# The context layer's matmuls in plain float32, and its weight chunks in one ring with the experts'

## The chip, the cores and the metric

One core of one Trainium2 chip runs the whole program. The metric is the time of one execution on the device in microseconds; the number given for a kernel is the median of its runs. A single execution, taken by the hardware profiler, gives the rows quoted below.

## What is computed

Two models follow one another on 256 tokens of width 1024, all in float32. The first block mixes (an mLSTM and a gated MLP), attends to a memory, and passes through a mixture of 32 experts. The second block runs two layers on that result (the "latent"), and each of them attends to a second sequence, the context, of 256 rows. The context itself passes through the first layer too, and through the key and value part of the second:

```python
x = first_block(...)                     # ... x + hier_moe(rms_norm(x)), 32 experts, top 2 of one group
xc = ctx
for l in range(2):
    x, xc = _layer(x, xc, ..., ctx_out=(l < 1))

# in _layer, for the context:
hc = rmsnorm(xc, norm_g) * (1.0 + scale_c) + shift_c
parts_c = _split_cols(hc @ w_in)         # layer 0: all 2816 columns; layer 1: only k and v
oc_att = silu(parts_c[3]) * _context_attention(qc, kc, vc)
oc_f, oc_c, oc_p = _local_branches(...)  # Fourier, convolution and pooling branches
xc = xc + gate_c * (concat([oc_f, oc_att, oc_c, oc_p]) @ w_out)

# an expert, on its tokens:
(silu(xb @ w_gate[e]) * (xb @ w_up[e])) @ w_down[e]
```

Nothing of the context's layer depends on the first block, so it can run at any time before the latent layers.

## The kernel before

The program has three parts in time: the first block's mixer and attention (to about 300 us), the experts (about 300 to 830 us), and the two latent layers.

**The experts.** Each pair of experts q has 12 chunks of 128x2048 float32 (1 MB): eight for the gate and up weights, four for the down weights. `SEQ` lists the 192 chunks in the order of use: seven units of two pairs (four experts, 32 columns of TensorE each) and two units of one pair. `expert_unit` multiplies gate and up chunks into tiles named `a` (function `hidden`), the down chunks into tiles named `py`. `moe_chunk` loads a chunk, as one transfer or as two of 512 KB, all from SyncE's queue, which issues in order and waits for the buffer's last user. `st_chunk` picks the buffer: for the first 46 chunks (`NROT`) out of up to 19 buffers, several of them in memory of the front part (pools `pm`, `pf`, `px`), which are given back after unit 1 (`LCU`). From chunk 46 on it rotates through eight buffers of the pool `st`: four with the tag `w`, two `wh`, two `wl`.

**Products in two parts.** Wherever accuracy allows no single reduced product, a float32 operand is written as high + low in the type float32r, and a product becomes three matmuls: high with high, high with low, low with high. For a weight chunk `wchunk` does this: a raw chunk (tag `w`), a high copy by ScalarE (tag `wh`, line 141), a low part by VectorE for one half (`wl`, line 143) and by GpSimd for the other (line 146). `split` does the same for small operands. `fm` and `tm` are the two matmul helpers: the weight chunk stationary, or the activations stationary; each does 48 matmuls of 256 columns for a chunk. The experts' matmuls are plain float32.

**The context's layer.** `gen_ctx` is a generator. `feed` advances it by small steps at fixed points of `expert_unit`, so that its work is spread over units 2 to 6; a planner that simulates a time line then sets the final order on each engine. It runs `layer` with s = 1, which the latent layers use with s = 0: `norm_mod` normalises and transposes the input, then come 11 chunks of `w_in2` and four of `w_out2`, one more chunk of layer 1 for its keys and values: 16 chunks of 1 MB. Each goes through `wchunk`, so it holds three of the eight `st` buffers. Its products land in tiles named `f`; the normalised input is `h2h`, `h2l`, the branches' results `y2h`, `y2l` (made by `put`).

Of the kernel before, what the change touches and what calls it, by code (L numbers as in the profile page):

```python
# [9 lines left out]
F32 = mybir.dt.float32  # L10
# [8 lines left out]
P = 128  # L19
# [8 lines left out]
NS = 4  # L28
NROT, LCU = 46, 1
D = 1024  # L30
KT = 8
# [14 lines left out]
def body(ctx: ExitStack, tc: tile.TileContext, I: dict, out: bass.AP, dbg=None):  # L46
# [156 lines left out]
    def fm(w, h, pst):  # L203

        (wh, wl), (hh, hl) = w, h
        p = pst([2, 256])
        for j in range(2):
            c = slice(j * P, (j + 1) * P)
            for k in range(KT):
                mm(p[:, j], wh[:, k, c], hh[:, k], k == 0, False)  # L210
                mm(p[:, j], wh[:, k, c], hl[:, k], False, False)
            for k in range(KT):
                mm(p[:, j], wl[:, k, c], hh[:, k], False, k == KT - 1)
        return p

    def tm(w, h, t, pst, ks=tuple(range(KT))):

        (wh, wl), (hh, hl) = w, h
        p = pst([wh.shape[2]])
        c = slice(t * P, (t + 1) * P)  # L220
# [434 lines left out]
    slots = [(pf, "p%d" % i) for i in range(NPF)] + [(pm, "mh"), (pm, "ml")]  # L655

    def st_chunk(i):
        n = i
        j = i % (NPF + NX + 10)
        if i < NROT and j >= 8:  # L660
            pool, t = slots[j - 8]
            return moe_chunk(*SEQ[i], pool, t, 1)
        i -= 0 if i >= NROT else i - j
        tag = ("w", "wh", "w", "wl")[i % 4]
        return moe_chunk(*SEQ[n], st, tag, 4 if tag == "w" else 2)

# [178 lines left out]
    def norm_mod(lp, src, l, s, pst, hi, lo, pre=None):  # L845

        ys = [lp.tile([P, D], F32, name="yn", tag="yn", bufs=2) for t in range(2)]
        if pre:
            for h in (slice(0, 512), slice(512, D)):
                for t in range(2):  # L850
                    last = nc.vector.tensor_scalar(ys[t][:, h], src[:, t, h], pre[0][t], None, op0=ALU.mult)
        else:
            for t, y in enumerate(ys):
                r = rms_scale(lp, src[:, t], hi[:, 4 * t:4 * t + 4].rearrange("p a b -> p (a b)"))
                nc.vector.tensor_scalar(y, src[:, t], r, None, op0=ALU.mult)
        sc_ = pre[1] if pre else mod_a[l][:, :, s]
        for f in range(KT):
            p = pst([256])
            for t in range(2):
                nc.tensor.transpose(p[:, t * P:(t + 1) * P], ys[t][:, f * P:(f + 1) * P], ident)  # L860
            a_, b_ = sc_[:, f:f + 1], mods[l][:, f, s:s + 1]
            ev = nc.scalar.activation(hi[:, f], p, AF.Identity, scale=a_, bias=b_)
            tf = lp.tile([P, 256], F32, name="tf", tag="gtm", bufs=2)
            if f % 2:
                nc.scalar.activation(tf, p, AF.Identity, scale=a_, bias=b_)
            else:
                nc.vector.tensor_scalar(tf, p, a_, b_, op0=ALU.mult, op1=ALU.add)
            ev2 = nc.vector.tensor_tensor(lo[:, f], tf, hi[:, f], op=ALU.subtract)
            if f == 7:
                late = (ev, ev2)  # L870
        after_norm[0] = ev2
        return [(last, *pre[2]), (pre[2][0], *late)] if pre else [(), ()]
# [36 lines left out]
    def hpair2(lp, n):  # L909
        return (lp.tile([P, KT, 256], F32R, name=n + "h", tag=n + "h"),  # L910
                lp.tile([P, KT, 256], F32R, name=n + "l", tag=n + "l"))

    def layer(lp, l, s, src, pst, ptr, pat, done=None, pre=None, res=None):
        lat = s == 0
        GC = GS = None
        if lat:
            gb, GC, GS = lrows[l], *rot
            if l:
                rope_rows(l, *rot)
        hT = hpair2(lp, "h2")  # L920
        chain = norm_mod(lp, src, l, s, ptr, *hT, pre=pre)
        yield
# [3 lines left out]
        for c in range(2):  # L926
            with ExitStack() as es:

                for i in chain[c] if c or l == 0 else ():
                    es.enter_context(tc.issue_after(i.ins))  # L930
                w = wchunk(w_in[c])
            for t in range(2):
# [6 lines left out]
        def zsilu(c):  # L939
            z = lp.tile([P, 2, 256], F32, name="sz", tag="sz", bufs=2)  # L940
            nc.scalar.activation(z, fm(wchunk(w_in[c]), hT, pst), AF.Silu)
            return z

        def half_sums(c):

            u = lp.tile([P, 2, 256], F32, name="u", tag="u")
            u0 = lp.tile([P, 256], F32, name="u0", tag="gtm", bufs=2)
            w = wchunk(w_in[c])
            nc.scalar.activation(u0, tm(w, hT, 0, pst), AF.Copy)
# [21 lines left out]
        nk = len(keys)  # L971
        yT = hpair2(lp, "y2")

# [4 lines left out]
        def put(f, val):  # L978

            n = val.shape[1]  # L980
            split(val, yT[0][:, f:f + n], yT[1][:, f:f + n])


        for j in range(2):
# [20 lines left out]
            nc.vector.tensor_tensor(sz[:, j], po, sz[:, j], op=ALU.mult)  # L1005
            yield
# [14 lines left out]
        for f in range(2):  # L1021
# [6 lines left out]
            for o, op in ((yf[:, f, 0:130], ALU.add), (yf[:, f, 127:257][:, ::-1], ALU.subtract)):  # L1028
                nc.vector.tensor_tensor(o.rearrange("p (m e) -> p e m", e=2), pc_, sn_, op=op)
        nc.vector.tensor_tensor(sz, yf[:, :, 0:256], sz, op=ALU.mult)  # L1030
        put(0, sz)
        yield

        p = fm(wchunk(w_in[3]), hT, pst)
        up = lp.tile([P, 2, 272], F32, name="up", tag="up")
# [31 lines left out]
        cg = lp.tile([P, 2, 256], F32, name="cg", tag="PT2", bufs=2)  # L1067
        nc.scalar.activation(cg, fm(wchunk(w_in[8]), hT, pst), AF.Copy)
        yield
        p = pst([2, 256])  # L1070
        for a in range(2):
            mm(p[:, a], pwb[l][:, a], dT[:, a], True, True)
            cp = C_PS2 + 2 * l + a
            nc.vector.scalar_tensor_tensor(sz[:, a], p[:, a], col[:, cp:cp + 1], sz[:, a],
                                           op0=ALU.mult, op1=ALU.mult)
        put(6, sz)
        p = fm(wchunk(w_in[9]), hT, pst)
        tp = lp.tile([P, 2, 258], F32, name="tp", tag="PT2", bufs=2)
# [17 lines left out]
        yield  # L1096
        p = fm(wchunk(w_in[10]), hT, pst)
        nc.vector.tensor_tensor(cg, p, cg, op=ALU.mult)
        put(4, cg)
        yield  # L1100
        sq = lp.tile([P, 2, 4], F32, name="sq")
        for c in range(4):
            w = wchunk(I["w_out2"][l, c])
            for t in range(2):
# [19 lines left out]
    def gen_ctx():  # L1124
# [6 lines left out]

        hT = hpair2(lp, "y2")
        norm_mod(lp, xc, 1, 1, psF, *hT, pre=pre)
        yield
        qkv = lp.tile([P, 2, 512], F32, name="qkv", tag="qkv")
        w = wchunk(I["w_in2"][1, 1])
        for t in range(2):
# [507 lines left out]
```

## Time and profile before

| | before |
|---|---|
| median of 3 runs | 1103.26 us (1099.52 to 1105.23) |
| profiled execution | 1105.26 us |
| its span, first to last instruction | 1103.4 us |
| TensorE busy | 1013.0 us (92%) |
| VectorE, ScalarE, GpSimd busy | 504.9, 372.3, 269.3 us |
| read from memory | 314.74 MB, 286 GB/s over the span |

Matmuls are pipelined and overlap, so TensorE's busy share is not a measure of its load: a matmul that is in the array while the next one starts counts for both. The throughput line in 40 slices of 27.6 us shows best which part is which: it stands near 409 GB/s for most of the experts' part, from slice 11 to slice 30. PE is TensorE, PEld its weight loads, DVE VectorE, ACT ScalarE, POOL GpSimd, SP SyncE; a q behind a name is that engine's queue.

### The profile page before, as it was taken

The numbers are of one execution on the slowest core, as the hardware profiler recorded it, in microseconds if no ns is written. First come the engines' busy times: TensorE is split into PE (matmuls) and PEld (weight loads), VectorE is DVE, ScalarE is ACT, GpSimd is POOL, SyncE is SP. The second block draws the span as 40 slices with busy tenths as digits, with TensorE's granted clock in tenths as the row PEclk, the third lists the DMA queues.
The fourth block names the chain that finished last, engine by engine and source line by source line (L and its number), as shares of the span: only waits on it lengthen the run. The fifth ranks groups of instructions, "written<-read, shape, count | busy, mean of one in ns | idle before, by whom it ended". The sixth has DMA issues, their size and how long they took to land.

```text
span 1103.4 us, 19306 instructions
## 1 busy us (share of the span) xinstructions
PE 1013.0 (92%) x7552; PEld 715.1 (65%) x7552; DVE 504.9 (46%) x992; ACT 372.3 (34%) x656; POOL 269.3 (24%) x211
## 2 busy tenths in 40 slices
PE   8999999999898588899989999997898889998998
PEld 7888999989651232643545654542235878988888
DVE  4966844353640141404432421513133777668755
ACT  5576445443100030211311221310014545554452
POOL 3245443234100000400220121111001453436233
PEclk9999999999799799999999999999999889999999
DMA  9657688866799999799679999999995432335231
GB/s 358 248 212 286 254 291 311 323 232 229 273 392 409 372 412 411 305 398 409 231 313 377 391 390 380 406 408 408 408 409 211 142 126 102 129 115 197 72 114 39
DMA packets 74456, 317.07 MB, mean 287 GB/s; under 512 B 8310, under 2 KB 10742, under 8 KB 61308
## 3 DMA queue, kind: packets, MB, share of 16 engines
q1 hardware_dynamic: 71480, 312.61, 74.0%
q10 hardware_dynamic: 2884, 3.21, 0.9%
q8 instruction: 60, 0.98, 0.4%
q14 instruction: 32, 0.26, 0.1%
HBM read 314.74 MB, written 1.05 MB: 286 GB/s over the span
## 4 chain that ended last, share of the span: by engine, by line
PE 33%; DMA 21%; issue 10%; DVE 4%; SPq 2%; POOL 2%; ACT 2%; DVEq 0%; POOLq 0%; ACTq 0%
DMA wm<-moe 21%; PE a L106 19%; PE f L106 7%; PE py L106 3%; PE sc L106 2%; SPq L543 2%; DVE wl L143 1%; PE po L106 1%; ACT wh L141 1%; POOL wl L146 1%; PE t L997 1%; PE t L860 0%; DVE qkv L885 0%; POOL rrow L906 0%; SPq L552 0%
## 5 line engine op out<-in xcount | busy, mean ns | idle before, releaser
L146 POOL TENSOR_TENSOR wl<-w,wh 128x512 fp32r<-128x512 f32 (+1 forms) x158 | 224.4, 1441 | 535.1 <-ACT wh L141 453.8
L106 PE MATMUL a<-wm,xg 128*32 128x512 f32 (+1 forms) x1024 | 219.4, 609 | 15.1 <-DMA wm<-moe 14.8
L141 ACT ACTIVATE wh<-w 128x1024 fp32r<-128x1024 f32 (+1 forms) x158 | 157.0, 1041 | 107.0 <-PE a L106 54.0
L143 DVE TENSOR_TENSOR wl<-w,wh 128x1024 fp32r<-128x1024 f32 (+1 forms) x79 | 107.4, 1359 | 87.6 <-ACT wh L141 86.0
L106 PEld LDWEIGHTS a<-wm,xg 128*32 128x32 f32 (+1 forms) x1024 | 46.8, 113 | 146.7 <-DMA wm<-moe 79.1
L106 PE MATMUL py<-wm,aT 128*32 128x256 f32 (+1 forms) x1024 | 90.1, 398 | 19.4 <-ACT aT L1389 12.6
L106 PEld LDWEIGHTS py<-wm,aT 128*32 128x32 f32 (+1 forms) x1024 | 41.1, 116 | 58.7 <-ACT aT L1389 14.1
L106 PE MATMUL a<-h2l,wh 128*128 128x256 f32 x256 | 67.1, 293 | 0.0
L106 PE MATMUL a<-h2h,wh 128*128 128x256 f32 x256 | 66.5, 292 | 0.0
L1382 DVE SCALAR_TENSOR_TENSOR sg<-a,ws,sg 128x512 f32<-128x512 f32 x9 | 6.8, 751 | 119.2 <-PE a L106 119.2
L106 PEld LDWEIGHTS a<-h2l,wh 128*128 128x128 f32 x256 | 49.6, 194 | 3.6 <-issue 3.5
L106 PEld LDWEIGHTS a<-h2h,wh 128*128 128x128 f32 x256 | 49.7, 194 | 0.8 <-issue 0.7
L106 PE MATMUL a<-hh,wh 128*128 128x256 f32 x192 | 49.0, 291 | 0.3 <-ACT wh L141 0.3
L106 PE MATMUL a<-hl,wh 128*128 128x256 f32 x192 | 47.8, 285 | 0.0
L1389 ACT ACTIVATE aT<-t 128x512 f32<-128x512 f32 x9 | 5.3, 592 | 110.2 <-PE t L1387 78.4
L106 PEld LDWEIGHTS a<-hh,wh 128*128 128x128 f32 x192 | 37.3, 194 | 2.6 <-ACT wh L141 1.7
L1415 DVE SCALAR_TENSOR_TENSOR yl<-py,ws,yh 128x512 fp32r<-128x512 f32 x16 | 12.0, 750 | 56.2 <-ACT yh L1414 56.2
L106 PE MATMUL a<-h2h,wl 128*128 128x256 f32 x256 | 37.7, 284 | 0.0
L106 PEld LDWEIGHTS a<-hl,wh 128*128 128x128 f32 x192 | 37.3, 194 | 0.0
L106 PE MATMUL f<-h2h,wh 128*128 128x256 f32 x128 | 32.8, 292 | 1.8 <-ACT wh L141 1.8
L106 PEld LDWEIGHTS a<-h2h,wl 128*128 128x128 f32 x256 | 33.4, 188 | 0.7 <-issue 0.7
L106 PE MATMUL a<-wh,yh 128*128 128x256 f32 x128 | 33.0, 292 | 0.0
(500 smaller groups left out, 2113.7 us busy)
## 6 DMA issues: line engine op xcount, KB each, us to landing
wm<-moe SPq DMA_DIRECT2D x336, 512.0 KB, 10.1
w<-w_in SPq DMA_DIRECT2D x46, 1024.0 KB, 5.2
w<-w_mod SPq DMA_DIRECT2D x24, 1024.0 KB, 5.0
wm<-moe SPq DMA_DIRECT2D x24, 1024.0 KB, 8.7
w<-w_out SPq DMA_DIRECT2D x16, 1024.0 KB, 5.0
w<-w_kv SPq DMA_DIRECT2D x8, 1024.0 KB, 5.0
w<-w_q SPq DMA_DIRECT2D x4, 1024.0 KB, 8.6
w<-w_o SPq DMA_DIRECT2D x4, 1024.0 KB, 7.1
```

The costliest lines, as they stand in the source:

```text
L106: return nc.tensor.matmul(o, l, r, start=a, stop=b)
L141: nc.scalar.activation(hi[:, a:a + n], raw[:, a:a + n], AF.Copy)
L143: nc.vector.tensor_tensor(lo[:, a:a + n], raw[:, a:a + n], hi[:, a:a + n], op=ALU.subtract)
L146: nc.gpsimd.tensor_tensor(lo[:, a:a + n], raw[:, a:a + n], hi[:, a:a + n], op=ALU.subtract)
L543: nc.sync.dma_start(t[:, e * 1024:(e + 1) * 1024], I["moe"][bass.ds(expert_at(2 * q + e), 1), c].rearrange("a p n -> p (a n)"))
L997: nc.tensor.transpose(pt[:, i], sm[:, i * P:(i + 1) * P], ident)
L1382: nc.vector.scalar_tensor_tensor(sg, pu, ws[:, 1:2], sg, op0=ALU.mult, op1=ALU.mult)
L1389: nc.scalar.activation(aT, pt, AF.Copy)
L1415: nc.vector.scalar_tensor_tensor(yl[:, cs], py[c], ws[:, 0:1], yh[:, cs], op0=ALU.mult, op1=ALU.subtract)
```

## The change

`fm` and `tm` get a second form: if the weight is a single tile, they do one plain float32 matmul where the other form does three. The context's layer uses it throughout: `norm_mod` writes one float32 tile instead of two parts, the branches write into one tile `y2` (`piece`, in place of `put`), and `fchunk` loads a chunk with no copies behind it. The latent layers keep the form in two parts.

`fchunk` takes its buffer from the same rotation as the experts' chunks (`ring`, with a shared counter `used`), and the rotation gets four more buffers, `r0` to `r3`, in memory that is free after unit 1. So there are 12, and a context chunk takes one.

```diff
+NRX = 4
     def fm(w, h, pst):
+        p = pst([2, 256])
+        if not isinstance(w, tuple):
+            for j in range(2):
+                for k in range(KT):
+                    mm(p[:, j], w[:, k, j * P:(j + 1) * P], h[:, k], k == 0, k == KT - 1)
+            return p
...
     def tm(w, h, t, pst, ks=tuple(range(KT))):
+        c = slice(t * P, (t + 1) * P)
+        if not isinstance(w, tuple):
+            p = pst([w.shape[2]])
+            for k in ks:
+                mm(p, h[:, k, c], w[:, k], k == ks[0], k == ks[-1])
+            return p
...
+    def ring(i):
+        if i >= NROT and i % (8 + NRX) >= 8:
+            return slots[-1 - i % (8 + NRX) + 8][0], slots[-1 - i % (8 + NRX) + 8][1], 1
+        i = i % (8 + NRX) if i >= NROT else i
+        tag = ("w", "wh", "w", "wl")[i % 4]
+        return st, tag, 4 if tag == "w" else 2
+
+    used = [NROT]
+
     def st_chunk(i):
-        n = i
         j = i % (NPF + NX + 10)
-        if i < NROT and j >= 8:
+        if i >= NROT:
+            used[0] += 1
+            return moe_chunk(*SEQ[i], *ring(used[0] - 1))
+        if j >= 8:
             pool, t = slots[j - 8]
             return moe_chunk(*SEQ[i], pool, t, 1)
-        i -= 0 if i >= NROT else i - j
-        tag = ("w", "wh", "w", "wl")[i % 4]
-        return moe_chunk(*SEQ[n], st, tag, 4 if tag == "w" else 2)
+        return moe_chunk(*SEQ[i], *ring(j))
+
+    def fchunk(src):
+        pool, tag, n = ring(used[0])
+        used[0] += 1
+        t = pool.tile([P, 2048], F32, name="wc", tag=tag, bufs=n)
+        nc.sync.dma_start(t, src)
+        return t.rearrange("p (k c) -> p k c", k=8)
...
+            if lo is None:
+                if f % 2:
+                    nc.scalar.activation(hi[:, f], p, AF.Identity, scale=a_, bias=b_)
+                else:
+                    nc.vector.tensor_scalar(hi[:, f], p, a_, b_, op0=ALU.mult, op1=ALU.add)
+                continue
...
+        wt = wchunk if lat else fchunk
...
-        hT = hpair2(lp, "h2")
+        hT = hpair2(lp, "h2") if lat else hone(lp, "h2")
...
-                w = wchunk(w_in[c])
+                w = wt(w_in[c])
...
         def put(f, val):
             n = val.shape[1]
-            split(val, yT[0][:, f:f + n], yT[1][:, f:f + n])
+            if lat:
+                split(val, yT[0][:, f:f + n], yT[1][:, f:f + n])
...
+        def piece(f, val):
+            return val if lat else yT[:, f:f + val.shape[1]]
...
         if u == LCU:
             pre.close()
+            rx = mo.enter_context(tc.tile_pool(name="rx", bufs=1, reuse_waits="tile"))
+            slots += [(rx, "r%d" % i) for i in range(NRX)]
```

How this moves the instructions, at three places. First TensorE, at the end of unit 2, where the context layer's first products stand. Of before; `wh` is a chunk's high part, `h2h` and `h2l` the two parts of the normalised context, and the rows with `f` go on in this way to 48 for a chunk:

```order
L1387 MATMUL t<-c_ident,sg 128x128 x4
L106 MATMUL t<-WRp,Pm 32x2 x8
L106 MATMUL py_4561<-wm,aT 32x256 x3
L1360 MATMUL t<-c_ident,Pm 128x128 x2
L106 MATMUL py_4561<-wm,aT 32x256 x29
L106 MATMUL f<-wh,h2h 128x256
L106 MATMUL f<-wh,h2l 128x256
```

The same place now; `wc` is a context chunk as loaded:

```order
L108 MATMUL py_4539<-wm,aT 32x256 x30
L108 MATMUL f<-wc,h_4412 128x256 x16
L108 MATMUL py_4540<-wm,aT 32x256
L108 MATMUL a<-yh,PT 128x512
L108 MATMUL a<-yl,PT 128x512
L108 MATMUL a<-yh,PT 128x512
L108 MATMUL f<-wc,h_4412 128x256 x16
L108 MATMUL py_4540<-wm,aT 32x256 x31
L108 MATMUL f<-h_4412,wc 128x256 x16
```

Each chunk's 48 matmuls have become 16, and they stand at the same points among the experts' matmuls.

Second SyncE, at the first context chunks and the expert chunk behind them, with what each load waits for (a DMAHW name is a place among the loads in flight, the others are engines that used the buffer before). Of before:

```order
L67 DMA w_4608<-w_in2 128x2048 [waits DMAHW5_49,PE_49]
L67 DMA w_4669<-w_in2 128x2048 [waits DMAHW6_49,PE_49]
L543 ISA
L543 DMA wm_4730<-moe 128x1024 [waits DMAHW7_49,PE_49]
L543 ISA
L543 DMA wm_4730<-moe 128x1024 [waits DMAHW0_49]
L543 ISA
L543 DMA wm_4733<-moe 128x1024 [waits DVE_49,PE_49,DMAHW1_49,Activation_49,Pool_49]
```

Now, at the same point of SyncE's order:

```order
L694 DMA wc_4586<-w_in2 128x2048 [waits DMAHW5_49,PE_49]
L694 DMA wc_4608<-w_in2 128x2048 [waits DMAHW6_49,PE_49]
L555 ISA
L555 DMA wm_4630<-moe 128x1024 [waits DMAHW7_49,PE_49]
L555 ISA
L555 DMA wm_4630<-moe 128x1024 [waits DMAHW0_49]
L555 ISA
L555 DMA wm_4633<-moe 128x1024 [waits DMAHW1_49,PE_49]
```

The loads stand in the same sequence, but an expert chunk behind a context chunk now waits for TensorE alone, not for the three engines that made its parts.

Third SyncE, at the context's input `xc`. Of before, at the end of unit 1's loads:

```order
L552 ISA x2
L1129 DMA xc_4406<-ctx 128x1024 [waits DMAHW7_49,PE_49]
L1129 DMA xc_4406<-ctx 128x1024 [waits DMAHW0_49]
L543 ISA
L543 DMA wm_4183<-moe 128x1024 [waits DMAHW1_49,PE_49]
```

Now, among unit 2's loads:

```order
L555 DMA wm_4398<-moe 128x1024 [waits DMAHW1_49]
L555 ISA
L555 DMA wm_4398<-moe 128x1024 [waits DMAHW2_49]
L1176 DMA xc_4409<-ctx 128x1024 [waits DMAHW3_49]
L1176 DMA xc_4409<-ctx 128x1024 [waits DMAHW4_49]
```

It has moved behind 14 expert chunks. Ahead of unit 1's end, and behind the last expert, each engine's instructions stand in the same order in both kernels.

## Rows read from the trace of the kernel before

**Rows 1.** The page: throughput in 40 slices; chain; loads, median us to landing

```profile
GB/s 358 248 212 286 254 291 311 323 232 229 273 392 409 372 412 411 305 398 409 231 313 377 391 390 380 406 408 408 408 409 211 142 126 102 129 115 197 72 114 39
DMA wm<-moe 21%; PE a L106 19%; PE f L106 7%; PE py L106 3%; PE sc L106 2%; SPq L543 2%; DVE wl L143 1%; PE po L106 1%; ACT wh L141 1%; POOL wl L146 1%; PE t L997 1%; PE t L860 0%; DVE qkv L885 0%; POOL rrow L906 0%; SPq L552 0%
wm<-moe SPq DMA_DIRECT2D x336, 512.0 KB, 10.1
```

**Rows 2.** Stretches: us, busy us per engine (instructions), granted clock, DMA share, GB/s

```profile
440.00:705.00 265.00, 242.11 (x1720) 140.26 (x1716) 81.49 (x164) 60.71 (x102) 45.67 (x32) 0.99 0.92 358
705.00:820.00 115.00, 103.94 (x620) 41.88 (x614) 32.67 (x76) 18.09 (x33) 8.57 (x9) 0.99 1.03 408
440.00:460.00 20.00, 18.17 (x147) 15.45 (x140) 8.11 (x13) 6.12 (x9) 7.42 (x5) 0.91 0.71 265
460.00:530.00 70.00, 62.85 (x400) 27.28 (x395) 20.27 (x60) 14.58 (x31) 6.49 (x5) 1.00 1.02 405
530.00:560.00 30.00, 28.93 (x230) 19.26 (x228) 12.65 (x23) 9.33 (x14) 6.11 (x4) 1.00 0.63 235
570.00:585.00 15.00, 13.53 (x102) 12.15 (x104) 3.45 (x4) 5.29 (x7) 6.05 (x4) 1.00 0.55 186
585.00:705.00 120.00, 111.26 (x822) 64.81 (x822) 35.60 (x62) 25.11 (x42) 19.59 (x14) 1.00 1.00 394
```

**Rows 3.** Waits of SyncE's queue, 440 to 705 us: total us, times, longest us

```profile
SPq L543 <- PE f L106: 66.2, 8, 14.2
SPq L543 <- PE a L106: 28.2, 13, 6.0
SPq L543 <- DMA wm<-moe: 27.4, 40, 1.5
SPq L543 <- PE py L106: 26.7, 7, 6.6
...
SPq L543 <- POOL wl L146: 5.7, 4, 2.2
```

**Rows 4.** The same view, 705 to 830 us

```profile
SPq L543 <- DMA wm<-moe: 52.5, 67, 2.1
```

**Rows 5.** The chain that ended last, about 536 to 570 us: start, us, what

```profile
536.78 3.90 ACT wh L141 x4
540.72 1.84 POOL wl L146
542.60 3.83 PE f L106 x30
...
550.36 5.00 PE f L106 x40
...
567.76 1.92 PE a L106 x10
```

**Rows 6.** TensorE in order of time, three places: start, us, operation, tiles, shape, count

```profile
453.80 0.87 PE L106 MATMUL f<-wl,h2h 128*128 128x256 f32 x6
...
387.20 1.89 PE L106 MATMUL f<-wf,k_bd 128*128 128x256 f32 x8
...
444.21 0.41 PE L106 MATMUL f<-wh,h2l 128*128 128x256 f32 x1
444.42 0.41 PE L106 MATMUL f<-wh,h2h 128*128 128x256 f32 x1
```

**Rows 7.** Raw chunks in 380 to 720 us: ns of one (min/median/max), first and last start

```profile
L141 ACT ACTIVATE wh<-w x32: 1040/1047/1062, 441.5 to 719.7; 128x1024 fp32r<-128x1024 f32 x32
L146 POOL TENSOR_TENSOR wl<-w,wh x30: 1266/1304/2337, 443.6 to 699.4; 128x512 fp32r<-128x512 f32 x30
L143 DVE TENSOR_TENSOR wl<-w,wh x16: 1214/1226/2206, 442.6 to 719.9; 128x1024 fp32r<-128x1024 f32 x16
```

**Rows 8.** ScalarE and VectorE in order of time, at the context's input

```profile
386.88 1.05 ACT L161 ACTIVATE h2h<-xc 128x1024 fp32r<-128x1024 f32 x1
...
391.31 0.75 DVE L855 TENSOR_SCALAR yn<-xc,rr 128x1024 f32<-128x1024 f32 x1 [0.67 <-POOL rr L124]
```

**Rows 9.** SyncE's queue in order of time, the last expert loads

```profile
790.38 35.93 SPq L543 DMA_DIRECT2D wm<-moe  x27
```

More of the change, by code (lines that the diff above doesn't have):

```diff
@@ L203, in fm @@
     def fm(w, h, pst):
+        p = pst([2, 256])
[4 more added lines that the diff above has]
+            return p
         (wh, wl), (hh, hl) = w, h
-        p = pst([2, 256])
         for j in range(2):
@@ L216, in tm @@
     def tm(w, h, t, pst, ks=tuple(range(KT))):
+        c = slice(t * P, (t + 1) * P)
[4 more added lines that the diff above has]
+            return p
         (wh, wl), (hh, hl) = w, h
         p = pst([wh.shape[2]])
-        c = slice(t * P, (t + 1) * P)
         for h0 in (ks[:6], ks[6:]):
@@ L870, in norm_mod @@
                 late = (ev, ev2)
+        if lo is None:
+            return [(), ()]
         after_norm[0] = ev2
@@ L911, in hpair2, with hone @@
                 lp.tile([P, KT, 256], F32R, name=n + "l", tag=n + "l"))
+    def hone(lp, n):
+        return lp.tile([P, KT, 256], F32, name=n, tag=n)
     def layer(lp, l, s, src, pst, ptr, pat, done=None, pre=None, res=None):
         lat = s == 0
+        wt = wchunk if lat else fchunk
         GC = GS = None
@@ L919, in layer @@
                 rope_rows(l, *rot)
-        hT = hpair2(lp, "h2")
-        chain = norm_mod(lp, src, l, s, ptr, *hT, pre=pre)
+        hT = hpair2(lp, "h2") if lat else hone(lp, "h2")
+        chain = norm_mod(lp, src, l, s, ptr, *(hT if lat else (hT, None)), pre=pre)
         yield
@@ L940, in zsilu @@
             z = lp.tile([P, 2, 256], F32, name="sz", tag="sz", bufs=2)
-            nc.scalar.activation(z, fm(wchunk(w_in[c]), hT, pst), AF.Silu)
+            nc.scalar.activation(z, fm(wt(w_in[c]), hT, pst), AF.Silu)
             return z
@@ L947, in half_sums @@
             u0 = lp.tile([P, 256], F32, name="u0", tag="gtm", bufs=2)
-            w = wchunk(w_in[c])
+            w = wt(w_in[c])
             nc.scalar.activation(u0, tm(w, hT, 0, pst), AF.Copy)
@@ L971, in layer @@
         nk = len(keys)
-        yT = hpair2(lp, "y2")
+        yT = hpair2(lp, "y2") if lat else hone(lp, "y2")
         def own(tag, shared, bufs=1):
@@ L1004, in layer @@
                     mm(po[64 * b:64 * b + 64], vals[i][:, 64 * b:64 * b + 64], PT[b][:, i], i == 0, i == 2 * nk - 1)
-            nc.vector.tensor_tensor(sz[:, j], po, sz[:, j], op=ALU.mult)
+            nc.vector.tensor_tensor(piece(2 + j, sz[:, j:j + 1])[:, 0], po, sz[:, j], op=ALU.mult)
             yield
@@ L1029, in layer @@
                 nc.vector.tensor_tensor(o.rearrange("p (m e) -> p e m", e=2), pc_, sn_, op=op)
-        nc.vector.tensor_tensor(sz, yf[:, :, 0:256], sz, op=ALU.mult)
+        nc.vector.tensor_tensor(piece(0, sz), yf[:, :, 0:256], sz, op=ALU.mult)
         put(0, sz)
         yield
-        p = fm(wchunk(w_in[3]), hT, pst)
+        p = fm(wt(w_in[3]), hT, pst)
         up = lp.tile([P, 2, 272], F32, name="up", tag="up")
@@ L1067, in layer @@
         cg = lp.tile([P, 2, 256], F32, name="cg", tag="PT2", bufs=2)
-        nc.scalar.activation(cg, fm(wchunk(w_in[8]), hT, pst), AF.Copy)
+        nc.scalar.activation(cg, fm(wt(w_in[8]), hT, pst), AF.Copy)
         yield
@@ L1073, in layer @@
             cp = C_PS2 + 2 * l + a
-            nc.vector.scalar_tensor_tensor(sz[:, a], p[:, a], col[:, cp:cp + 1], sz[:, a],
+            nc.vector.scalar_tensor_tensor(piece(6 + a, sz[:, a:a + 1])[:, 0], p[:, a], col[:, cp:cp + 1], sz[:, a],
                                            op0=ALU.mult, op1=ALU.mult)
         put(6, sz)
-        p = fm(wchunk(w_in[9]), hT, pst)
+        p = fm(wt(w_in[9]), hT, pst)
         tp = lp.tile([P, 2, 258], F32, name="tp", tag="PT2", bufs=2)
@@ L1096, in layer @@
         yield
-        p = fm(wchunk(w_in[10]), hT, pst)
-        nc.vector.tensor_tensor(cg, p, cg, op=ALU.mult)
+        p = fm(wt(w_in[10]), hT, pst)
+        nc.vector.tensor_tensor(piece(4, cg), p, cg, op=ALU.mult)
         put(4, cg)
@@ L1102, in layer @@
         for c in range(4):
-            w = wchunk(I["w_out2"][l, c])
+            w = wt(I["w_out2"][l, c])
             for t in range(2):
@@ L1130, in gen_ctx @@
         _, pre = yield from layer(lp, 0, 1, xc, psF, psF, psF, res=xc)
-        hT = hpair2(lp, "y2")
-        norm_mod(lp, xc, 1, 1, psF, *hT, pre=pre)
+        hT = hone(lp, "y2")
+        norm_mod(lp, xc, 1, 1, psF, hT, None, pre=pre)
         yield
         qkv = lp.tile([P, 2, 512], F32, name="qkv", tag="qkv")
-        w = wchunk(I["w_in2"][1, 1])
+        w = fchunk(I["w_in2"][1, 1])
         for t in range(2):
```

## The prediction

> **What bounds the kernel now.** I read the throughput line of the page first [rows 1]: between slices 11 and 30 it stands near 409 GB/s, except in a few slices, the deepest 231 and 313. This is the experts' stage, 16 pairs of experts streamed as 192 chunks of 1 MB, and the chain that ended last gives the experts' loads 21% of the span [rows 1], the largest single item. The windows [rows 2] cut the stage. From 705 to 820 us, where but one chunk of the context's layer is left, the 16 DMA engines are full: share 1.03, 408 GB/s. From 440 to 705, where the context's layer runs between the experts, they are not: share 0.92, 358 GB/s. The holes are in a few places: 440 to 460 at 0.71, 530 to 560 at 0.63, 570 to 585 at 0.55; 460 to 530 is full (1.02), and a remainder lies in 585 to 705 (394 GB/s).
>
> Next, who makes the holes: SyncE's own waits [rows 3]. In 440 to 705 its queue stands 66.2 us for TensorE's context matmuls (tile f) against 27.4 us for earlier loads. In 705 to 830 the order is turned round [rows 4]: loads 52.5 us, which is what a full DMA looks like, since SyncE holds eight loads of 512 KB in flight.
>
> The chain shows one hole from inside [rows 5]. At 536.78 TensorE stops for ScalarE, which makes the high parts of two chunks (3.90 us), then for GpSimd's low parts, then runs context matmuls from 542.60 to 555.36. From 536.78 to 555.36 are 18.6 us in which few expert buffers come free; SyncE stands, and TensorE then waits for its data until 567.76, when the expert matmuls start again. So the bound is the DMA stream, and what empties it is that buffers come back late.
>
> **Why they come back late.** A chunk is 1.049 MB, at 408 GB/s 2.57 us. A load lands 10.1 us after issue [rows 1], so four chunks are in flight. The ring has 8 buffers: TensorE may be late by 8 x 2.57 - 10.1 = 10.5 us before the DMA starves. A context chunk takes three of the eight (raw, high, low), and two in a row take six. 18.6 us of lateness cannot be covered.
>
> **The change part by part.**
>
> *Deeper ring, one buffer for a context chunk.* With 12 buffers the bearable lateness is 12 x 2.57 - 10.1 = 20.7 us, and a context chunk costs one place. In the new order TensorE takes the expert and context chunks almost exactly as SyncE issues them; one context chunk alone (the pool branch's input) stands four chunks behind its place. So no matmul stands before an older chunk's in a way that holds the ring. Nothing but SyncE's limit on loads in flight is then late next, and that is the full DMA. Gain, from two bounds: by share 265 x (1 - 0.92/1.03) = 28.3 us, by bytes 265 x (1 - 358/408) = 32.5 us [rows 2]. I take 30, between them, because the share counts the holes and the bytes also some slower packets that may remain, and give 1 us back for the start of the layer, when the four new buffers have not all come round: 29 us. Ends: 0 and 32.5.
>
> *Plain float32 matmuls.* A chunk had 48 matmuls of 256 columns, start to start (0.87 - 0.28)/5 = 0.118 us at 2.4 GHz [rows 6], 5.7 us; now it has 16. The nearest row is a full 128x128 float32 weight with 256 columns: 8 in 1.89 us [rows 6], (1.89 - 0.38)/7 = 0.216 us, so 3.5 us a chunk. Fifteen chunks lie in the stage: 85 us of TensorE become 52. Bounds: below, 0.118 us each (28 us); above, 0.43 us, the same at the lower clock (two rows at 444 us show 0.21 us start to start for the float32r kind [rows 6], twice 0.118, so twice 0.216; 104 us). None of these is on the path while the DMA is full: the eight expert matmuls of two chunks cost at most 1.54 us (10 in 1.92 [rows 5]) and two chunks take 5.1 us to land. A context chunk of 3.5 us makes TensorE late by 0.9 us, two in a row by under 2; even 6.9 us is far under 20.7. I count 0 for it. If that cover were gone the 33 us would come on top of the gain.
>
> *What the Trainium skill says against it.* The rows give a float32 matmul 0.216/0.118 = 1.8 times the time of a float32r one. The Trainium skill, "FP8 and Floating Point Precision", TensorE Precision Notes, says that true FP32 takes four passes through the array. By that rule 16 matmuls would be 64 passes against 48, 7.5 us a chunk, and TensorE's 85 us would grow to 113 instead of falling to 52. The trace of before disagrees on this shape, so the 52 stands.
>
> *The splits that go.* Per chunk two ScalarE copies of 1.05 us, one VectorE subtraction of 1.23, two GpSimd ones of 1.30 [rows 7], 16 times; with them the splits of the normalised input and of the branches' results, and the waits between the engines. As engine time they were beside other work (ScalarE busy 60.7 us of 265 in this stretch, GpSimd 45.7 [rows 2]); as a wait they are the first 5.8 us of each hole, already counted above. So 0 by themselves.
>
> *The context's input comes later.* Its two 512 KB loads move back 14 chunks in SyncE's queue and wait there for no engine, only for a place in flight; they hold nothing up behind them. The chain from them to the normalised rows is 386.88 to 392.06 us, 5.2 us [rows 8]; in the new order the transposes stand among the expert matmuls right after that landing, so TensorE may stand about 5 us there, with later chunks landed behind it. Covered by the ring (on its first round it goes 10 back: 10 x 2.57 - 10.1 = 15.6 us); uncovered it would be 5.
>
> *The rest.* Two chunks of unit 1 go to other buffers, and would at most let loads start sooner: 0. The four new buffers lie in memory that unit 1 has given back: its last chunks are consumed before the ring reaches them; 0, at worst one chunk, 2.6 us. Everything ahead of unit 1's end and behind the last expert stands in the same order on every engine: 0; the last four ring places are the same four tags as before, so the latent layers' first loads find their buffers as now.
>
> **Sum.** The profiled execution took 1105.26 us (span 1103.4). Its last expert load is issued at 826.31 [rows 9] and all that follows shifts with it. 1105.26 - 29 = 1076.3. The median of the three runs is 2.0 us under that execution, so the forecast in terms of the median is 1074 us.
>
> **The rivals.**
>
> *Half of it stays.* SyncE's waits in the stage also name the experts' own matmuls: 28.2 us for a, 26.7 for py [rows 3]. If these are the softmax chains and the dispatch at unit boundaries, which remain, only the part named by f and by the splits goes: (66.2 + 5.7)/(66.2 + 28.2 + 26.7 + 5.7) = 57% of 29, 16 us: 1087. Against it: units after 705 have the same boundaries, the same eight buffers and a share of 1.03 [rows 2].
>
> *Nothing on the end.* The holes close, but the bytes are the same and the DMA, shared with TensorE's reads, runs slower when full, or the ring does not get its depth because the first round's memory is held: 1103. For it: the 585 to 705 stretch shows share 1.00 and only 394 GB/s [rows 2]. Against it: 460 to 530 of the same stage runs full at 405 GB/s, and the stretch after it holds 408 [rows 2].
>
> *TensorE becomes the bound (slower).* Place: the same 265 us. Experts: 75 chunks there, 38 pairs at 1.54 us, 58 us. With the splits gone TensorE is less busy, and if it stood at 1.2 GHz the experts would cost 117 us. The matmuls would then have to cost over (265 - 117)/240 = 0.62 us each to lose time. Four times 0.21 us is 0.84, 202 us, with 117 makes 319: 54 us slower, 1157. The rule of the Trainium skill quoted above is what would bring this about, and only at the lower clock: at 2.4 GHz four passes are 0.47 us and stay hidden. Against it: the 0.216 us row, and 705 to 820, where experts alone keep a granted clock of 0.99, the 2.4 GHz level [rows 2].
>
> **How the numbers follow.** Full recovery 0.74 (1074; with its bounds 1069 to 1081), half 0.15 (1087), nothing 0.06 (1103), slower 0.05 (1157). Range 1068 to 1088: it holds the first case and the middle of the second, 0.8 or a little more. A measurement of this kernel tells about 0.5% (5.5 us) from no change. Faster by more: 0.74 + 0.15 = 0.89; same 0.06; slower 0.05.
>
> **What would show it.** In the changed kernel's windows the stretch from 440 us to the end of the context's layer should show share 1.02 to 1.03 and about 408 GB/s; SyncE's waits there should name loads, not the tile f; a context chunk's 16 matmuls should take about 3.5 us; the last expert load should be issued near 797 us instead of 826; what comes after it should be as long as before (about 277 us to the end). If holes stay at unit boundaries, the second case; if chunks of 16 take 7 us or more, the skill's rule; if the last load is early but the end is not, something behind it that I call unchanged is not.

## The result

The changed kernel takes 1067.06 us (median of four runs, 1065.75 to 1068.04) where the kernel before takes 1104.12 (four runs beside it, 1099.52 to 1105.23): a ratio of 0.967, with an interval of 0.964 to 0.970. It is faster by 37 us. The forecast was 29 us, 1074, with a range from 1068 to 1088; the time lies 0.94 us under it. The profiled execution took 1066.4 us, span 1064.6, against 1105.26 and 1103.4 before.

### The profile page after: what moved, and what is told of

It is laid out like the page before. It is cut to its first block, busy times and chain, and to the rows that moved or that the text cites. A ratio compares the mean times of both kernels' runs of the same rounds, so it can differ in the third digit from the quotient of the medians.

```text
span 1064.6 us, 18603 instructions
## 1 busy us (share of the span) xinstructions
PE 993.1 (93%) x7296; PEld 711.6 (67%) x7296; DVE 475.5 (45%) x956; ACT 332.5 (31%) x604; POOL 223.9 (21%) x179
## 4 chain that ended last, share of the span: by engine, by line
PE 35%; DMA 22%; issue 10%; DVE 4%; POOL 1%; SPq 1%; ACT 0%; DVEq 0%; POOLq 0%; ACTq 0%
PE a L108 19%; DMA wm<-moe 17%; PE f L108 8%; DMA wc<-w_in 3%; PE py L108 3%; PE sc L108 2%; PE po L108 1%; DMA wc<-w_out 1%; DVE wl L145 1%; PE t L1044 1%; POOL wl L148 1%; PE t L890 0%; SPq L564 0%; DMA wf<-w_four 0%; POOL rrow L944 0%
## 5 line engine op out<-in xcount | busy, mean ns | idle before, releaser
L148 POOL TENSOR_TENSOR wl<-w,wh 128x512 fp32r<-128x512 f32 (+1 forms) x126 | 179.1, 1441 | 266.8 <-ACT wh L143 234.4
L108 PE MATMUL a<-wm,xg 128*32 128x512 f32 (+1 forms) x1024 | 191.3, 607 | 8.3 <-DMA wm<-moe 8.0
L143 ACT ACTIVATE wh<-w 128x1024 fp32r<-128x1024 f32 (+1 forms) x126 | 125.1, 1038 | 79.3 <-PE a L108 41.2
L108 PEld LDWEIGHTS a<-wm,xg 128*32 128x32 f32 (+1 forms) x1024 | 44.2, 113 | 123.4 <-issue 68.1
L145 DVE TENSOR_TENSOR wl<-w,wh 128x1024 fp32r<-128x1024 f32 (+1 forms) x63 | 84.2, 1336 | 41.4 <-ACT wh L143 39.9
L108 PE MATMUL py<-wm,aT 128*32 128x256 f32 (+1 forms) x1024 | 85.9, 393 | 17.5 <-ACT aT L1436 11.1
L108 PE MATMUL f<-h,wc 128*128 128x256 f32 x256 | 57.0, 381 | 0.0
L108 PEld LDWEIGHTS f<-h,wc 128*128 128x128 f32 x256 | 48.1, 190 | 9.3 <-issue 2.5
L1467 DVE TENSOR_TENSOR x<-a,x 128x512 f32<-128x512 f32 x32 | 21.0, 686 | 36.7 <-PE a L108 36.7
```

Source lines behind the costliest of these rows:

```text
L108: return nc.tensor.matmul(o, l, r, start=a, stop=b)
L143: nc.scalar.activation(hi[:, a:a + n], raw[:, a:a + n], AF.Copy)
L145: nc.vector.tensor_tensor(lo[:, a:a + n], raw[:, a:a + n], hi[:, a:a + n], op=ALU.subtract)
L148: nc.gpsimd.tensor_tensor(lo[:, a:a + n], raw[:, a:a + n], hi[:, a:a + n], op=ALU.subtract)
L1467: nc.vector.tensor_tensor(x[:, t, cs], p, x[:, t, cs], op=ALU.add)
```

## The profile after

The page first: throughput in 40 slices (26.6 us each now), the chain that ended last, and the loads of expert chunks (KB each, median us to landing), which answer to [rows 1].

```profile
GB/s 353 274 200 277 251 305 321 296 259 218 230 389 408 408 373 415 416 415 414 415 415 418 417 416 416 415 411 405 414 393 120 159 83 118 157 103 212 62 101 40
PE a L108 19%; DMA wm<-moe 17%; PE f L108 8%; DMA wc<-w_in 3%; PE py L108 3%; PE sc L108 2%; PE po L108 1%; DMA wc<-w_out 1%; DVE wl L145 1%; PE t L1044 1%; POOL wl L148 1%; PE t L890 0%; SPq L564 0%; DMA wf<-w_four 0%; POOL rrow L944 0%
wm<-moe SPq DMA_DIRECT2D x336, 512.0 KB, 10.2
```

The deep slices are gone: from slice 15 to slice 25, counted from 0, none is under 414. The windows show it by stretch (columns as in [rows 2]); the context's layer now ends at 668 us instead of 705.

```profile
440.00:668.00 228.00, 221.50 (x1465) 137.38 (x1465) 57.31 (x145) 29.57 (x70) 2.67 (x2) 1.00 1.02 416
530.00:560.00 30.00, 30.00 (x175) 20.58 (x174) 7.51 (x20) 3.71 (x8) 0.00 (x0) 1.00 1.02 416
570.00:585.00 15.00, 14.16 (x93) 7.78 (x93) 4.47 (x11) 0.60 (x1) 0.00 (x0) 1.00 1.02 415
668.00:783.00 115.00, 105.74 (x608) 42.88 (x607) 29.23 (x68) 11.92 (x20) 5.97 (x7) 1.00 1.02 412
```

The two worst holes, 235 and 186 GB/s in [rows 2], are at 416 and 415. The loads that took 265 us take 228 (94.9 MB in either stretch). SyncE's waits in that stretch (total us, times, longest us):

```profile
SPq L555 <- DMA wm<-moe: 97.1, 133, 1.7
SPq L555 <- DMA wc<-w_in: 18.8, 10, 3.1
SPq L694 <- DMA wm<-moe: 11.7, 13, 0.9
SPq L555 <- DMA wc<-w_out: 7.4, 4, 1.9
SPq L555 <- PE f L108: 5.1, 2, 4.9
SPq L555 <- PE a L108: 2.7, 5, 1.4
SPq L555 <- PE py L108: 2.5, 6, 0.7
```

In [rows 3] the largest line was TensorE's tile f with 66.2 us; it is 5.1 now, and the queue waits for earlier loads, as it did before only behind the layer [rows 4]. The last expert loads in SyncE's order of time (start, us, operation):

```profile
671.84 112.86 SPq L555 DMA_DIRECT2D wm<-moe  x88
```

The last is issued at 784.7 us instead of 826.3 [rows 9]. The last expert matmul ends at 807.85 instead of 846.73, and from there to the end of the span both kernels take the same: 256.8 and 256.7 us. So all of the gain was made in the experts' stage. The two profiled executions are 38.9 us apart: 37 are the stretch above, and the faster DMA on either side of it makes, by its rates, 1.8 more (411 GB/s for 406 from 380 to 440 us, 412 for 408 behind the layer). From the last issue to the end are 279.9 us, against 277.1 before: with 12 places loads are issued further ahead of their use, so that sign of the forecast is off by 2.8 us without a change in the work behind.

One thing in this profile contradicts the forecast outright. The first row is TensorE in order of time, one context chunk; the others are groups of matmuls in 440 to 668 us (count; ns of one, min/median/max; first and last start).

```profile
460.30 7.17 PE L108 MATMUL f<-h,wc 128*128 128x256 f32 x32
...
L108 PE MATMUL f<-h,wc x256: 377/379/483, 460.3 to 616.7; 128*128 128x256 f32 x128
...
L108 PE MATMUL f<-wc,y x128: 379/379/483, 621.1 to 665.8; 128*128 128x256 f32 x128
...
L108 PE MATMUL f<-wc,h x96: 378/379/483, 441.2 to 486.0; 128*128 128x256 f32 x96
```

A chunk has 16 matmuls, and the stretch holds 15 chunks: 240. The trace has 256 + 128 + 96 = 480 records. A plain float32 matmul leaves two records, and the pair takes 7.17/16 = 0.45 us by this row, about 0.43 from start to start (two chunks in a row, shown further below, take 14.08 us, so the second adds 6.91/16): not the 0.216 of the forecast, and 3.7 times the 0.118 of a float32r one. The layer's matmuls take about 15 x 7.1 = 106 us of TensorE, where they took 85. The change made TensorE's work larger, and the kernel faster.

## The experiments

The kernel before, run beside each group, took 1103.8 to 1104.1 us. What is to be split up is the 37 us: into the ring's depth, the one place of a context chunk in place of three, and the products' form; and the shortfall of the forecast, 8 us.

**A ring of 8 and of 10.** The changed kernel with fewer of the new buffers.

```diff
-NRX = 4
+NRX = 0      # ring8;  ring10: NRX = 2
```

> The changed kernel with no extra buffers: the rotation has 8 buffers, a context chunk takes one of them, plain float32 matmuls stay. Theory 1 (depth): the rate of a full DMA, 416 GB/s in the changed kernel against 408 before, comes from loads that never start late, so with 8 buffers (10.5 us of bearable lateness) the stretch from 440 us on falls back to about 408 GB/s with small holes, and the time is 1071 to 1080 us. Theory 2 (traffic): the rate rose because the splits' reads and writes are gone from the on-chip memory; then 8 buffers keep 414 to 416 GB/s and the time stays within 2 us of the changed kernel (1065 to 1069). Theory 3 (most of the gain is the four extra buffers): above 1085.

> The changed kernel with two extra buffers in place of four (10 in the rotation). Theory 1 (depth): between the 8 and the 12, 1067 to 1072 us. Theory 2 (traffic): as the changed kernel, 1065 to 1069. If already 8 buffers are as fast as 12, this one is too.

Measured: 1076.8 us with 8 (ratio 0.976, 0.972 to 0.980), 1069.2 with 10 (0.9685, 0.9645 to 0.9725). The windows of the two, first 8, then 10:

```profile
440.00:668.00 228.00, 221.38 (x1454) 132.95 (x1447) 54.70 (x140) 28.74 (x66) 2.66 (x2) 1.00 1.01 403
680.00:780.00 100.00, 89.54 (x521) 36.46 (x514) 21.59 (x48) 9.88 (x17) 5.27 (x6) 1.00 1.03 409
```

```profile
440.00:668.00 228.00, 221.12 (x1460) 136.28 (x1460) 56.05 (x143) 29.36 (x68) 2.66 (x2) 1.00 1.02 412
680.00:780.00 100.00, 90.40 (x495) 37.18 (x494) 20.24 (x45) 8.10 (x14) 5.27 (x6) 0.95 1.03 412
```

SyncE's waits for TensorE with the ring of 8 in 440 to 668 us:

```profile
SPq L555 <- PE a L108: 26.3, 12, 4.8
SPq L555 <- PE f L108: 25.7, 8, 5.6
SPq L555 <- PE py L108: 9.9, 9, 4.4
```

Theory 1 of the ring of 8 holds. So 27 of the 37 us come without a single new buffer, the first two new buffers bring 7.6, and the last two 2. With 8 places the queue still waits 62 us for TensorE, in short pieces, the longest 5.6 us; before, one piece was 14.2 us [rows 3].

**One place, products in two parts.** A ring of 8, a context chunk takes one place in it, and high and low parts go to two tiles of their own; the products are those of the kernel before.

```diff
-NRX = 4
+NRX = 0
     def fchunk(src):
...
-        return t.rearrange("p (k c) -> p k c", k=8)
+        hi = lcp[0].tile([P, 2048], F32R, name="ch", tag="ch", bufs=1)
+        lo = lcp[0].tile([P, 2048], F32R, name="cl", tag="cl", bufs=1)
+        for a in (0, 1024):
+            nc.scalar.activation(hi[:, a:a + 1024], t[:, a:a + 1024], AF.Copy)
+        nc.vector.tensor_tensor(lo[:, 0:1024], t[:, 0:1024], hi[:, 0:1024], op=ALU.subtract)
+        for a in (1024, 1536):
+            nc.gpsimd.tensor_tensor(lo[:, a:a + 512], t[:, a:a + 512], hi[:, a:a + 512], op=ALU.subtract)
+        return hi.rearrange("p (k c) -> p k c", k=8), lo.rearrange("p (k c) -> p k c", k=8)
```

> Ring of 8, a context chunk takes one place of it, and its products are made in two parts as in the kernel before (high and low parts in two tiles of their own, one buffer each). Against the ring of 8 with plain float32 (1076.8 us) it tests the products alone, against the kernel before (1104) the one place for three. A chunk's raw buffer is free after the splits (4 to 5 us) and TensorE has 5.7 us of work for it instead of 7.1. Theory 1 (places in the ring decide): most of the gain of the ring of 8 stays, 1076 to 1085, with a few us lost where two chunks follow each other and the second waits for the tiles of the first. Theory 2 (the splits' waits are what held the buffers, the plain product is what gives the gain): 1092 to 1104.

Measured: 1084.3 us (0.982, 0.978 to 0.986). The window, and SyncE's waits in it:

```profile
440.00:668.00 228.00, 210.18 (x1554) 123.60 (x1547) 73.67 (x149) 55.71 (x92) 38.56 (x28) 0.99 0.97 381
```

```profile
SPq L555 <- PE py L108: 27.2, 7, 8.6
SPq L555 <- PE a L108: 24.2, 13, 5.4
SPq L694 <- PE a L108: 14.1, 4, 5.3
SPq L555 <- DVE cl L699: 11.9, 6, 4.2
SPq L555 <- POOL cl L701: 10.5, 6, 2.2
```

Theory 1 holds, at the upper end of its range: 20 of the 37 us come from one place in place of three, with the old products and eight places in the ring. The parts have not gone, though: they lie in two tiles beside the ring, so this kernel has the memory of two chunks more than the one before, and the 20 us are the price of holding ring places with the parts. The plain products bring the next 7.5 us (the four runs of the one and of the other do not overlap), although TensorE's part in them is longer. These rows, beside those of the ring of 8, show two waits that the splits make (`cl`, 22.4 us) and that the plain form does not have. So the splits' waits are not free by themselves, where the forecast counted 0. How much of the 7.5 us is theirs is not shown, for another wait comes from the single tile: of all waits from 440 to 668 us,

```profile
ACT ch L698 <- PE f L108: 10.6, 2, 5.8
```

that is, twice ScalarE's copy of a chunk waits until TensorE is done with the chunk before it. Two sets of these tiles might have kept a part of the 7.5; that was not tried.

The plain form also needs less memory. With the parts, the layer needs four tiles more (`ch`, `cl`, and the second halves of `h2` and `y2`), each of 2048 elements of 4 bytes per partition, as much as the four buffers `r0` to `r3`. Neither a ring of 12 with parts beside it nor one with three places a chunk was tried, so the shares of the 37 us hold for the order in which they were taken: one place, plain products, buffers.

**The splits' work alone.** The ring of 10, with the five split operations done again for each context chunk, into tiles that nothing reads (`jh`, `jl`, `jm`).

```diff
+        for a in (0, 1024):
+            nc.scalar.activation(hi, t[:, a:a + 1024], AF.Copy)
+        nc.vector.tensor_tensor(lo, t[:, 0:1024], hi, op=ALU.subtract)
+        for a in (1024, 1536):
+            nc.gpsimd.tensor_tensor(lo2, t[:, a:a + 512], hi[:, a - 1024:a - 512], op=ALU.subtract)
```

> Ring of 10, and for each context chunk the five split operations of the kernel before are done again (two ScalarE copies, one VectorE and two GpSimd subtractions) into tiles that nothing reads; the products stay plain float32. Compared with the ring of 10 alone (1069.2 us). Theory 1 (depth and places decide, the splits cost only as waits): a chunk's buffer now also waits for the splits, 1.05 + 1.05 + 1.23 or 2 x 1.30 us, mostly beside the 7.1 us of its matmuls: 1068 to 1073. Theory 2 (the splits' traffic in the on-chip memory is what held the DMA at 403 to 408 GB/s): the stretch from 440 to 668 us falls from 412 to about 405 GB/s, 4 us longer, and GpSimd's waits add to it: 1073 to 1080.

Measured: 1070.2 us (0.971, 0.967 to 0.975), against 1069.2 without them. Its window:

```profile
440.00:668.00 228.00, 221.46 (x1462) 136.48 (x1460) 78.37 (x159) 58.67 (x98) 53.78 (x32) 1.00 1.02 411
```

VectorE, ScalarE and GpSimd work 22, 29 and 51 us more than in the ring of 10, and the DMA keeps 411 GB/s to 412. As traffic and as engine time the splits cost nothing that can be measured.

**How far TensorE is from the bound.** Four kernels with the context's products made longer or shorter; nothing else changes. The first two do every product twice and four times.

```diff
-                for k in range(KT):
+                for k in list(range(KT)) * 2      # mm2;  mm4: * 4
...
-            for k in ks:
+            for k in list(ks) * 2:
```

> The changed kernel with every context matmul done twice into the same sum (512 float32 matmuls more of TensorE time 16 x 0.216 = 3.5 us a chunk, 55 us in all; the context's products come out doubled). Theory: TensorE is hidden behind the full DMA, a chunk's 32 matmuls take 6.9 us, time within 3 us of the changed kernel (1065 to 1070). Rival: TensorE is on the path, then 20 to 55 us more (1087 to 1122).

> The changed kernel with every context matmul done four times (a chunk 64 x 0.216 = 13.8 us; 0.86 us for what one matmul does; 166 us more in all). This is the price at which the prediction's slower rival put TensorE at its limit. Theory: two chunks in a row make TensorE late by 2 x 13.8 - 5.1 = 22 us, just over the 20.7 us that 12 buffers bear, so small holes: 1068 to 1090 us. Rival (TensorE on the path already): over 1170.

Measured: 1151.5 us (1.043, 1.039 to 1.048) and 1358.6 (1.232, 1.226 to 1.237). The first theory missed both times, by 80 us and more. The rival holds for the fourfold kernel (over 1170), and for the doubled one the time lies 29 us above its range. All four rested on the 0.216 us, which led to the count of records above. Windows of the doubled and of the fourfold one:

```profile
440.00:668.00 228.00, 224.98 (x1403) 160.79 (x1395) 42.98 (x115) 24.10 (x51) 2.66 (x2) 0.99 0.81 319
```

```profile
440.00:668.00 228.00, 226.09 (x1288) 169.17 (x1287) 28.17 (x79) 16.77 (x39) 2.66 (x2) 1.00 0.62 244
```

At 0.43 us, 256 more matmuls are 110 us and 768 are 332; 84 and 291 us were lost. The clock is full in both. So TensorE is the bound there, and some 26 to 41 us of its work had been hidden, an estimate. The next two ask where the limit lies: half of the eight k left out, and two of the eight done twice.

```diff
-                for k in range(KT):
+                for k in range(4):                             # mmhalf
+                for k in [0, 1, 2] + list(range(1, KT)):       # mm125
...
-            for k in ks:
+            for k in ks[:4]:                                   # mmhalf
+            for k in tuple(ks[:3]) + tuple(ks[1:]):            # mm125
```

> The changed kernel with four of the eight k in each context product left out: 8 matmuls a chunk instead of 16, some 55 us of TensorE less if one costs 0.43 us, 28 if 0.216. Theory 1 (DMA full, TensorE hidden): 1064 to 1067, no more than 2 us under the changed kernel, and SyncE's waits for f vanish. Theory 2 (TensorE already carries a part of the stage): 1055 to 1062.

> The changed kernel with two of the eight k in each context product done twice: 20 matmuls a chunk instead of 16, 64 x 0.43 = 27 us more of TensorE. From the doubled (110 us added, 84 lost) and the fourfold one (332 added, 291 lost) the slack of TensorE is some 26 to 41 us. Theory 1 (slack about 26 us or more): 1066 to 1072. Theory 2 (a chunk's own length counts, since it holds the ring while it runs, not the sum): a quarter of the doubled kernel's loss, 21 us: 1085 to 1090.

Measured: 1067.2 us (0.967, 0.963 to 0.971) with half, 1074.8 (0.974, 0.970 to 0.978) with a quarter more. Windows of the half:

```profile
440.00:668.00 228.00, 207.59 (x1284) 98.06 (x1276) 59.53 (x151) 30.00 (x70) 3.52 (x3) 1.00 1.02 416
```

With 55 us less on TensorE the stretch keeps its 416 GB/s and the kernel its time: in the changed kernel the products are wholly hidden. A quarter more, 27.6 us, loses 7.7, between the two theories. Its window around the loss, and the matmuls there:

```profile
550.00:560.00 10.00, 10.00 (x59) 6.32 (x58) 4.35 (x13) 1.28 (x2) 0.00 (x0) 1.00 0.44 153
```

```profile
545.89 8.90 PE L108 MATMUL f<-h,wc 128*128 128x256 f32 x40
554.73 3.63 PE L108 MATMUL a<-wm,xg 128*32 128x512 f32 x28
558.28 17.53 PE L108 MATMUL f<-h,wc 128*128 128x256 f32 x80
```

Three context chunks follow each other with 3.6 us of experts between them, 30 us in which TensorE takes few expert chunks out of the ring. In the changed kernel the same three take 24.7 us:

```profile
538.63 7.17 PE L108 MATMUL f<-h,wc 128*128 128x256 f32 x32
545.73 3.64 PE L108 MATMUL a<-wm,xg 128*32 128x512 f32 x32
549.30 14.08 PE L108 MATMUL f<-h,wc 128*128 128x256 f32 x64
```

There is no hole behind them (416 GB/s in 530 to 560, above). So the limit is set by how chunks are bunched as well as by the sum, and the change stands less than a quarter of the products' price from it.

**What sets the rate of the full DMA.** The rate rose with the ring even where the DMA is full (680 to 780 us, share 1.02 to 1.03): 408 GB/s before, 409 with 8, 412 with 10 and 12. So once more a ring of 8, but of other buffers: the four new ones in turn with the four of tag `w`.

```diff
+        if i >= NROT and i % 2:
+            return slots[-1 - i % 8 // 2][0], slots[-1 - i % 8 // 2][1], 1
+        if i >= NROT:
+            return st, "w", 4
```

> A ring of 8 again, but of other buffers: the four new ones (r0 to r3) in turn with the four of tag w, in place of w, wh, w, wl. Everything else as the changed kernel. It asks what raises the rate of the full DMA from 408 to 410 GB/s (ring of 8) to 415 (ring of 12): the number of buffers or the memory that they lie in. Number: 680 to 780 us and 455 to 525 us at 409 GB/s as in the ring of 8 before, 1075 to 1079 us. Memory: 412 and over in both stretches, with the holes between 560 and 610 us as in the ring of 8, 1071 to 1075 us.

Measured: 1076.6 us (0.975, 0.970 to 0.980). Its windows:

```profile
440.00:668.00 228.00, 219.82 (x1400) 130.09 (x1403) 53.29 (x136) 27.82 (x63) 2.66 (x2) 1.00 0.99 398
680.00:780.00 100.00, 90.23 (x559) 38.05 (x559) 24.89 (x56) 10.54 (x19) 5.96 (x7) 1.00 1.03 418
```

The two theories each get half. The rate follows the buffers, not their number: 418 GB/s with 8, more than with 12. The time follows the number: in the context's stretch the holes are as in the other ring of 8 or worse (398), and it ends where that one ended. In the records of the DMA's packets the rates are two prices: the median of the 128 packets of 4 KB in a load is 159 ns in every load of this ring from 700 us to the end of the stage, 162 to 164 in most loads of the ring of 8 old buffers, and in the changed kernel 159 for the new buffers and for the three old ones behind them, up to 164 for most of the other five.

That suggests another order of the twelve, a new buffer at every third place, run beside the changed kernel once more.

```diff
+        if i >= NROT and i % 3 == 1:
+            return slots[-1 - i % 12 // 3][0], slots[-1 - i % 12 // 3][1], 1
+        i = i % 12 // 3 * 2 + (i % 3 == 2) if i >= NROT else i
```

> The changed kernel once more, beside the next run: 1066 to 1068 us; 412 GB/s in 680 to 780 us.

> The changed kernel with the twelve buffers in another order: the new ones r0 to r3 at every third place (w, r0, wh, w, r1, wl, w, r2, wh, w, r3, wl) in place of eight old and then four new. With the ring of 8 old buffers the stretch from 680 to 780 us ran at 409 GB/s, with 8 of which every second one is new at 418, with 12 in the order of the changed kernel at 412. Theory 1 (loads into a new buffer, and those in flight beside them, are quicker): every four loads in flight then hold a new one, so 416 to 418 in 680 to 780 and 417 to 418 in 440 to 668; some 2 us sooner by the first and 1 to 2 by the second and the stretch after it: 1062 to 1065. Theory 2 (the share of new buffers alone counts): as the changed kernel, 412 and 416, 1066 to 1068.

Measured: 1065.8 us for the changed kernel again (0.9652, 0.9625 to 0.9679) and 1065.0 for the other order (0.9643, 0.9616 to 0.967). Windows of the other order:

```profile
440.00:668.00 228.00, 221.43 (x1475) 135.54 (x1474) 56.05 (x142) 29.23 (x67) 2.66 (x2) 1.00 1.02 417
680.00:780.00 100.00, 90.65 (x519) 37.94 (x519) 23.38 (x53) 9.82 (x17) 5.26 (x6) 0.98 1.02 414
```

The rate goes up a little in both stretches (416 to 417, 412 to 414), less than expected: the packets of 4 KB over 161 ns fall from 21% to 12% in 680 to 780 us and do not vanish. 0.8 us cannot be told from nothing. Nothing that was tried clearly beats the changed kernel.

## Why the prediction was right in direction and short in size

**The bound and its cause: right.** The DMA stream bounds the stage, and late buffers made its holes. The signs named for it came: share 1.02, waits that name loads, the last load far earlier. Two of them came larger than forecast, 416 GB/s for 408 and 41.6 us for 29.

**The deeper ring: right mechanism, its parts not told apart.** The forecast put "12 buffers" and "one place" into one term, 29 us, and counted 0 for the products. The runs split the 37: 20 us from one place in place of three, 7.5 from the plain products at 8 places, 9.7 from the four buffers. The formula for the lateness that the ring can bear (10.5 us at 8, 20.7 at 12) fits: at 8 the holes are smaller but stay, at 12 they are gone.

**The size of the gain: the step that failed.** The term for the deeper ring, "29 us. Ends: 0 and 32.5", was too small: it measured 37. By bytes, the stretch of before moved 265 us x 358 GB/s = 94.9 MB [rows 2]. At the 408 of the forecast that is 232.5 us, at the 416 measured 228: a gain of 37, not 32.5. The 408 was the rate that the kernel before shows where it is full, taken as the most that could be had; with other buffers the same loads run at up to 418, as the second ring of 8 shows. This is 4.5 of the 8 us. Another 2.5 went with the choice of 30, between the share and the bytes: the bytes were the right measure, and a share of 1.03 at 408 and of 1.02 at 416 shows that the share cannot see how long a packet takes. The last 1 us was given back for the start of the layer, which runs at 415 (440 to 530 us). The range reached down to 1068 on the same 408, so its end failed with it. That the stretch and the medians both give 37 is in part chance: the profiled executions are 38.9 us apart, 1.9 of them outside the stretch, and the one of before was 1.1 us over its median, the one of the changed kernel 0.7 under.

**The price of a float32 matmul: wrong by a factor of two, without effect on the time.** The forecast read "x8" in [rows 6] as eight matmuls. There are four in the program at that place, two records each, so the row gives 0.43 us and not 0.216. The forecast's own sign for the other reading, chunks of 16 that take 7 us or more, came with 7.17. The Trainium skill, "FP8 and Floating Point Precision", TensorE Precision Notes, with its four passes for true FP32, was set aside in the forecast on the strength of that row. The traces agree with it: 7.1 us a chunk against 7.5, an estimate from its four passes, 64 of 0.118 us. The same slip is in the price of the experts: "10 in 1.92" [rows 5] are five matmuls, and in the changed kernel the 32 records of four chunks take 3.64 us (above), so two chunks cost 1.8 and not at most 1.54; against the 5.1 us of their loads that changes nothing. The wrong price did not move the time because the forecast had a second leg: even 6.9 us a chunk would be far under the 20.7 that the ring bears. The half product shows that leg to be right. But the margin was much thinner than the text had it.

**TensorE as the bound: a limit that came near by luck.** The rival meant slower than the kernel before, and put the limit for that at 0.62 us a matmul, with the experts at the half clock. That premise did not come: the granted clock is 1.00 in the whole stretch, the 2.4 GHz level. With the experts at the forecast's 58 us for the full clock, the same formula gives (265 - 58)/240 = 0.86. At just that price, 2 x 0.43, the doubled kernel is 47 us slower than the one before, so the formula alone puts the limit too high. On a straight line between it and the kernel with a quarter more (0.43 x 1.25 = 0.54, 1074.8 us) the time of before is reached at about 0.66, an estimate. The formula counts experts and context products alone, as a sum over the stage, and misses that chunks come in bunches. The room under the changed kernel's own time is smaller: at 0.54 already 7.7 us are lost, which leaves about 27.6 - 7.7 = 20 us of slack if each further us costs one, again an estimate.

**The splits: right as work, open as waits.** They cost nothing as work (ring of 10 with and without, 1.0 us apart, inside either interval). As waits the forecast took the first 5.8 us of the hole at 536.78 [rows 5] as time in which TensorE stops. TensorE in order of time shows that context matmuls had begun again by 538.30:

```profile
538.30 0.28 PE L106 MATMUL f<-h2h,wh 128*128 128x256 f32 x1
```

A row of the chain says what the last of them hung on, not that the engine stood. That the splits' waits can hold places is seen with the parts beside the ring of 8 (`cl`, above); their share in the old holes was not measured by itself.

**The context's input, the first round, the tail: right.** From 380 to 440 us, where `xc` now comes, the DMA keeps 411 GB/s (406 before); the tail is the same to 0.1 us. "Half of it stays" and "nothing on the end" fell: no line of SyncE's waits for a or py is over 2.7 us now, and the full DMA ran at 416 GB/s beside TensorE's larger work, not under 408.

## What to carry to other kernels

Where transfers are the bound and their buffers come back late, count the places that one piece of work takes in the ring before counting the engines' work: here one place in place of three was worth 20 us and four new buffers after it 9.7. A form that costs TensorE a quarter more time still gained 7.5, since TensorE was hidden and the splits' waits went; how far it could go is another matter, for a quarter more again would have cost 7.7. Before a row's count is used as a number of instructions, hold it against the program's own count at that place. And a rate read from a kernel as "full" is that kernel's full rate; a range that rests on it needs room above it.

## What the runs showed of the hardware

A plain float32 matmul with a full 128x128 weight and 256 columns shows as two records in the trace (480 for 240), and costs about 0.43 us at a granted clock of 1.00, against 0.118 for one of kind float32r, which leaves one.

By the median of a load, a 4 KB packet of a saturated stream takes 159 ns or up to 164 ns, and which of the two depends here on the buffers that are loaded together: 418 GB/s against 409 for the same loads in the same order, 8 buffers each, with the same engines at work. The buffers of tag `w` occur in both rings, so it is no property of one buffer alone. What makes it stays open.
